# High halves of the weight tiles: a rounding DMA from GpSimd in place of a GpSimd instruction

## The chip, the cores and the metric

One core of one Trainium2 chip runs the whole program. The metric is the device time of one execution in microseconds; the median of several runs is compared. A profile is one more execution, recorded instruction by instruction.

## What is computed

One layer of a streaming encoder, for 512 prompt tokens and 32 sample tokens together (544 columns, model width 1024):

```python
z = rmsnorm(x, n1) @ w_in              # 52 tiles of 128 features: q, k, v of mixers A and B, gates
mixed = sigmoid(ga) * attend_A(...) + sigmoid(gb) * attend_B(...)   # 16 heads each
x = x + mixed @ w_out
u = rmsnorm(x, n2) @ w_up              # 2 x 2816 features
a, g = split(causal_conv3(u))
x = x + (gelu(a) * g) @ w_down
```

All of it is float32, and the products have to keep most of float32's precision.

## The kernel before

Each weight matrix is cut into tiles of 128 rows by 1024 columns (eight blocks of 128 by 128): 52 tiles of `w_in`, 8 of `w_out`, 44 of `w_up` and 22 of `w_down`, 126 in all, used one after the other in a fixed order. TensorE takes operands of a rounded type (float32r). To keep precision each operand is split into a high half (the value rounded) and a low half (the rest), and one block of weights costs three products: high weights with high activations, high weights with low activations, low weights with high activations (`triple`). With two column halves of 272 and eight blocks, one weight tile is 48 products.

`prep(n)` makes the two halves of tile n. SyncE (its queue is SP) loads the tile into `w_raw`; GpSimd (POOL in the profile) multiplies it by one into `w_hi`, whose type rounds (L193); VectorE (DVE) subtracts to get `w_lo` (L194). There are two buffers each of `w_raw`, `w_hi` and `w_lo`. So `w_hi` of tile n can be written only when TensorE has read the high half of tile n-2 for the last time, and TensorE can start tile n only when the new half is there:

```python
raw = wp.tile([128, 1024], F32, name="w_raw", bufs=2)
hi = wp.tile([128, 1024], F32R, name="w_hi")
lo = wp.tile([128, 1024], F32R, name="w_lo")
```

`weights()` takes the next tile and has up to two further ones prepared ahead of it in program order. The first two tiles come in two pieces each.

The program has four stages. In the first, tiles of `w_in` are projected while heads of both mixers, in steps, are woven between the products by the class `Stream`; every step of a head has work on ScalarE (ACT), VectorE and GpSimd, GpSimd doing the normalization of the softmax (L483) and the squares of the head norms (L403, L404, L411). Then come `w_out`, `w_up` (with a convolution per tile: L925, L932, L937 on VectorE, and four instructions of one or two columns on GpSimd, L928 to L935) and `w_down`. Within each engine the instructions stand in the order that a list scheduler gave them when the program was built; at run time each engine takes them strictly in that order, and an instruction that waits holds up everything behind it on its engine.

Of the kernel before, what the change touches and what calls it, by code (L numbers as in the profile page):

```python
# [11 lines left out]
ALU = mybir.AluOpType  # L12
# [3 lines left out]
NP = 512                 # prompt tokens  # L16
NS = 32                  # sample tokens
T = NP + NS              # columns of the activations
# [4 lines left out]
CA = 128                 # cached keys of mixer A  # L23
CB = 256                 # cached keys of mixer B
FF = 2816
UT = 2 * FF // 128       # tiles of the up projection
# [3 lines left out]
A_BLK = 80               # sample keys of mixer A: 2 blocks of 80 (32 new, 128 cached)  # L30
B_BLK = 96               # sample keys of mixer B: 3 blocks of 96 (32 new, 256 cached)
LN_EXP = "natural_log_exp_and_others"

# tiles of w_in, 128 output features each
QA, KA, VA, QB, KB, VB, GA, GB = 0, 8, 10, 12, 20, 28, 36, 44

# columns of the packed per-feature vectors
# [11 lines left out]
# how long the operands of a task's next step take, in the units of Stream.clock  # L49
LAT_FIRST, LAT_ROW = 9.15, 0.35          # the norm of the columns, before w_in and before w_up  # L50
LAT_SQ, LAT_NORM, LAT_DMA = 2.9, 6.89, 3.63
LAT_Z, LAT_SOFT, LAT_PT = 6.55, 9.34, 4.75
LAT_SOFT_S, LAT_PTS = 8.46, 1.1          # the sample's
PACE_A, PACE_B, PACE_S = 7.09, 5.87, 1.44

WARM = 7                 # products that bring the tensor engine's clock up
START = "x0a w0 x0b x1 w1 x2 w0 x3 w1 x4 x5 x6 x7"   # first loads: rows of x (or halves), parts of w
FIRST = 3                # tiles of w_in whose products go ahead of the norm
RESCALE = 8              # tiles of w_in whose moving operand is without the norm
GATES_B = (1, 2, 12, 12)  # before which group of A (0-3) or pair of B (4-11) the gates of B come  # L60
LATER = -300             # the priority of work that others can go ahead of


class Stream:
    """The order of the tensor engine's work: products are queued as they are emitted, and tasks
    (generators that yield how long their next step's operands take) resume between them.  Heads
    wait in a queue until their projections are there, one of them starting every PACE."""
# [24 lines left out]
    def queue(self, fetch, start, needs, pace, ahead=0):  # L92
        """a head: what to load ahead, the task, and when its operands are there; it goes
        before the last `ahead` ones"""
        self.heads.insert(len(self.heads) - ahead, [fetch, start, needs, None, pace])
        self.prefetch()

    def reserve(self, name, n, limit):
        """let tasks go on until n more of a group of buffers can be had"""
        while self.live.get(name, 0) + n > limit:  # L100
            self.idle()
        self.live[name] = self.live.get(name, 0) + n
# [15 lines left out]
    def step(self):  # L118
        """resume one task whose operands are there, or start a head"""
# [19 lines left out]
def body(ctx, tc, a, o):  # L139
# [21 lines left out]
    def load(out, src, kind="x"):  # L161
        """loads of a kind are issued in the order in which they are asked for"""
        with tc.issue_after(loads[kind].ins) if kind in loads else nullcontext():
            loads[kind] = nc.sync.dma_start(out=out, in_=src)

    # ---------------------------------------------------------------- weights
# [18 lines left out]
    def prep(n):  # L185
# [5 lines left out]
        for c in map(slice, cuts, cuts[1:]):  # L191
            load(raw[:, c], sources[n][:, c])
            G.tensor_scalar(hi[:, c], raw[:, c], 1.0, 1.0, ALU.mult, ALU.mult)  # L193
# [16 lines left out]
    def triple(ps, w, k, c0, cn, first, last):  # L210
        """the products of one block of weights: high x high, high x low, low x high"""
# [27 lines left out]
    def rescale(n, s, k):  # L239
        """the columns' norm goes into the moving operand: the tiles after RESCALE have it"""  # L240
# [13 lines left out]
    def interleaved(halves, ks):  # L254
        """row by row"""
# [5 lines left out]
    def dense_first(evac):  # L261
        """the first tiles of a stage: their products start as the rows come in, and they
        leave their banks when the norm of the columns is there"""
# [13 lines left out]
    def leave(z, ps, c0, cn):  # L277
        """from a bank, with the norm if the moving operand was without it"""
# [5 lines left out]
    # -------------------------------------------------------------- constants  # L284
# [16 lines left out]
    # ------------------------------------------------------------------ norms  # L301
    def newton(st, cn, pool):
        """(b - 3) y = -2 / sqrt(st + eps)"""
# [16 lines left out]
    class RowNorm:  # L320
        """the reciprocal root mean square of every column, of rows that come one by one"""
# [38 lines left out]
    # products without a use, until the first rows are there: they bring the clock up  # L360
# [29 lines left out]
    # -------------------------------------------------------- projected tiles  # L390
# [38 lines left out]
    def load_q(stacks, sample, ready):  # L429
        """stacks: per head of the pair a [128, 512] tile of high and low halves"""  # L430
# [11 lines left out]
    def load_v(vt, vs, cached, vt_out, c_out, ready):  # L442
        """vt[token, tile, head, (high, low), feature]; vs[key, block, head, feature] for the sample"""
# [23 lines left out]
    # -------------------------------------------------------------- attention  # L467
    def softmax(p, tiles, mx, sinkcol):
        """tiles: slices of p holding scores whose row maxima are the columns of mx"""
# [24 lines left out]
    def transposed(p, blocks, n):  # L494
        """blocks: (column in p, column in the result); returns high and low parts of p^T"""
# [609 lines left out]
```

## Time and profile before

| | us |
|---|---|
| median of 3 runs | 934.55 (932.86 to 937.06) |
| span of the profiled execution, first to last instruction | 931.9 |
| TensorE products busy | 905.8 (97%) |
| TensorE weight loads busy | 891.7 (96%) |
| VectorE busy | 656.7 (70%) |
| GpSimd busy | 467.0 (50%) |
| ScalarE busy | 445.1 (48%) |

The profiled execution's own time is its span, 931.9 us; what a run has around the span is not recorded for it, and the median of the runs is 2.65 us above it. Busy time of TensorE is the time in which at least one product is under way; products overlap one another, so a busy TensorE need not be one at its full rate. Only idle time of the engine that sets the end counts; the other engines' idle time costs nothing by itself.

### The profile page before, as it was taken

How to read it: one execution, taken by the hardware profiler on the slowest of the kernel's cores; microseconds unless marked ns; L12 is line 12 of the kernel's file. 1: busy time of each engine (PE TensorE's matmuls, PEld its weight loads, DVE VectorE, ACT ScalarE, POOL GpSimd, SP SyncE). 2: the span in 40 equal slices, each digit the busy share in tenths (PEclk: the TensorE clock that was granted, in tenths of full speed). 3: DMA queues.
4: the chain of work that ended last, by engine and by line, in shares of the span. 5: the costliest groups of instructions: out<-in, count | busy, mean ns of one | idle time of the engine just before them, and what ended most of it. 6: DMA issues, size and time to landing. Idle time of an engine off the chain costs nothing.

```text
span 931.9 us, 18669 instructions
## 1 busy us (share of the span) xinstructions
PE 905.8 (97%) x7181; PEld 891.7 (96%) x7181; DVE 656.7 (70%) x1243; ACT 445.1 (48%) x1103; POOL 467.0 (50%) x636
## 2 busy tenths in 40 slices
PE   7979999999999999999999999999999999999998
PEld 6878999989989999999999999999999999999998
DVE  7798867777988988989766568777777777422221
ACT  5667887778878687777672232222222222000000
POOL 5625548366777677766451146544555554311110
PEclk9999999999999999999999999999999999999999
DMA  6222123312344344334324222222222222333321
GB/s 220 89 91 83 52 95 99 103 59 83 109 145 128 98 138 128 127 110 125 107 86 169 89 70 91 91 91 91 91 84 80 87 92 91 107 103 103 113 90 40
DMA packets 39000, 94.35 MB, mean 101 GB/s; under 512 B 4832, under 2 KB 14336, under 8 KB 38912
## 3 DMA queue, kind: packets, MB, share of 16 engines
q1 hardware_dynamic: 38912, 93.17, 31.1%
q8 instruction: 56, 0.92, 0.4%
q14 instruction: 32, 0.26, 0.1%
HBM read 80.48 MB, written 7.10 MB: 94 GB/s over the span
## 4 chain that ended last, share of the span: by engine, by line
PE 78%; DVE 8%; ACT 3%; POOL 3%; issue 2%; DMA 0%; DVEq 0%; POOLq 0%; ACTq 0%
PE ps L80 75%; PE ps L84 3%; DVE q L436 1%; ACT p L475 1%; DVE w_lo L194 1%; DVE p L491 1%; POOL p L483 1%; DVE zn L412 1%; DVE s L244 1%; DVE t_b L309 1%; POOL t_sql L404 1%; DVE k L421 0%; POOL z L411 0%; DVE xl L317 0%; DMA k<-k 0%
## 5 line engine op out<-in xcount | busy, mean ns | idle before, releaser
L80 PE MATMUL ps<-xh,w_lo 128*128 128x272 f32 x1536 | 444.4, 290 | 5.9 <-DVE w_lo L194 5.8
L80 PE MATMUL ps<-xh,w_hi 128*128 128x272 f32 x1536 | 444.1, 291 | 3.4 <-ACT z L402 1.6
L80 PE MATMUL ps<-xl,w_hi 128*128 128x272 f32 x1536 | 444.2, 290 | 1.3 <-DVE xl L317 1.2
L80 PEld LDWEIGHTS ps<-xh,w_lo 128*128 128x128 f32 x1536 | 289.4, 189 | 7.6 <-DVE w_lo L194 7.0
L80 PEld LDWEIGHTS ps<-xh,w_hi 128*128 128x128 f32 x1536 | 289.7, 189 | 4.9 <-ACT z L402 1.9
L80 PEld LDWEIGHTS ps<-xl,w_hi 128*128 128x128 f32 x1536 | 289.8, 189 | 2.6 <-DVE xl L317 2.1
L193 POOL TENSOR_SCALAR w_hi<-w_raw 128x1024 fp32r<-128x1024 f32 (+2 forms) x128 | 137.5, 1074 | 288.8 <-PE ps L80 178.2
L194 DVE TENSOR_TENSOR w_lo<-w_raw,w_hi 128x1024 fp32r<-128x1024 f32 (+2 forms) x128 | 162.4, 1270 | 105.6 <-POOL w_hi L193 105.2
L80 PE MATMUL ps<-s,w_hi 128*128 128x272 f32 x960 | 180.6, 288 | 0.0
L80 PEld LDWEIGHTS ps<-s,w_hi 128*128 128x128 f32 x960 | 150.4, 188 | 0.0
L80 PE MATMUL ps<-s,w_lo 128*128 128x272 f32 x480 | 137.8, 288 | 0.0
L483 POOL TENSOR_SCALAR p<-p,rc 128x256 f32<-128x256 f32 (+3 forms) x128 | 74.5, 598 | 43.3 <-DVE rc L481 39.9
L80 PEld LDWEIGHTS ps<-s,w_lo 128*128 128x128 f32 x480 | 90.2, 188 | 0.0
L475 ACT ACTIVATE p<-p,nm 128x256 f32<-128x256 f32 (+3 forms) x128 | 65.4, 513 | 27.8 <-DVE nm L472 27.7
L925 DVE TENSOR_TENSOR u<-ps,rstd 128x272 f32<-128x272 f32 x88 | 38.2, 438 | 38.8 <-PE ps L80 38.2
L420 ACT CAST s<-s 128x544 fp32r<-128x544 f32 x30 | 19.4, 647 | 84.9 <-DVE s L950 81.5
L80 PE MATMUL ps<-k,q 128*128 128x256 f32 (+2 forms) x256 | 52.1, 308 | 3.3 <-DMA k<-k 1.6
L404 POOL TENSOR_TENSOR t_sql<-t_sq,t_sqh 128x272 fp32r<-128x272 f32 x52 | 52.6, 1011 | 3.7
L411 POOL TENSOR_TENSOR z<-z,t_y 128x272 f32<-128x272 f32 x52 | 42.6, 821 | 21.9 <-ACT t_y L306 19.9
L931 ACT ACTIVATE s<-u,cols 128x544 f32<-128x544 f32 x44 | 36.9, 842 | 34.0 <-DVE u L925 34.0
L945 ACT ACTIVATE s<-s 128x544 f32<-128x544 f32 x22 | 14.5, 658 | 75.5 <-DVE s L937 75.5
L403 POOL TENSOR_SCALAR t_sqh<-t_sq 128x272 fp32r<-128x272 f32 x52 | 29.9, 575 | 39.4 <-ACT t_sq L401 34.7
(129 smaller groups left out, 1340.9 us busy)
## 6 DMA issues: line engine op xcount, KB each, us to landing
w_raw<-in_w_in SPq DMA_DIRECT2D x50, 512.0 KB, 3.3
w_raw<-in_w_up SPq DMA_DIRECT2D x44, 512.0 KB, 3.2
w_raw<-in_w_down SPq DMA_DIRECT2D x22, 512.0 KB, 3.2
k<-k SPq DMA_DIRECT2D x40, 128.0 KB, 2.3
bias<-in_rel SPq DMA_DIRECT2D x16, 256.0 KB, 2.7
w_raw<-in_w_out SPq DMA_DIRECT2D x8, 512.0 KB, 3.3
s<-in_x SPq DMA_DIRECT2D x15, 272.0 KB, 5.6
out_vb<-s SPq DMA_DIRECT2D x8, 272.0 KB, 2.3
```

Of the source, the lines that this page charges most:

```text
L80: return self.nc.tensor.matmul(out, lhsT=lhsT, rhs=rhs, **kw)
L84: return self.nc.tensor.transpose(out, src, ident)
L193: G.tensor_scalar(hi[:, c], raw[:, c], 1.0, 1.0, ALU.mult, ALU.mult)
L194: V.tensor_tensor(lo[:, c], raw[:, c], rr(hi)[:, c], ALU.subtract)
L403: G.tensor_scalar(sqh, sq, 1.0, 1.0, ALU.mult, ALU.mult)
L404: G.tensor_tensor(sql, sq, rr(sqh), ALU.subtract)
L411: G.tensor_tensor(z, z, y, ALU.mult)
L420: nc.scalar.copy(dst_hi, src)
L475: act(p[:, sl], p[:, sl], AF.Exp, bias=nm[:, t:t + 1], accum_out=sm[:, t:t + 1])
L483: G.tensor_scalar(p[:, sl], p[:, sl], rc[:, t:t + 1], 1.0, ALU.mult, ALU.mult)
L925: V.tensor_tensor(u[:, 2 + c0:2 + c0 + cn], ps, rstd2[:, c0:c0 + cn], ALU.mult)
L931: act(c, u[:, 0:T], AF.Identity, scale=col("cw0", m), bias=col("cb", m))
```

## The change

`load` gets an argument for the issuing engine. For every tile from the fifth on (`CAST = 4`), `w_hi` is no longer computed by GpSimd from `w_raw`: a second DMA, issued from GpSimd, reads the same tile from memory again and writes it into `w_hi`, rounding to float32r on the way. The DMAs of this kind keep their order among themselves. VectorE's subtraction is as before and now waits for the second DMA in place of the GpSimd instruction. The first four tiles are untouched (six GpSimd instructions, two whole and four in pieces). The diff's other lines only take out comments, so from line 200 on the changed kernel's line numbers are 4 higher, and TensorE's products (L80) stand one line lower.

```diff
+CAST = 4
...
-    def load(out, src, kind="x"):
+    def load(out, src, kind="x", e=nc.sync):
         with tc.issue_after(loads[kind].ins) if kind in loads else nullcontext():
-            loads[kind] = nc.sync.dma_start(out=out, in_=src)
+            loads[kind] = e.dma_start(out=out, in_=src)
...
             load(raw[:, c], sources[n][:, c])
-            G.tensor_scalar(hi[:, c], raw[:, c], 1.0, 1.0, ALU.mult, ALU.mult)
+            if n < CAST:
+                G.tensor_scalar(hi[:, c], raw[:, c], 1.0, 1.0, ALU.mult, ALU.mult)
+            else:
+                load(hi[:, c], sources[n][:, c], "cast", G)
             V.tensor_tensor(lo[:, c], raw[:, c], rr(hi)[:, c], ALU.subtract)
```

The scheduler places instructions anew. In the stage of `w_up`, on VectorE, the order before is this (`u` is the evacuated product of one tile, in two halves; two `u` buffers take turns; L932 and L937 are the convolution):

```order
1087 L925 TENSOR_TENSOR u_8049<-ps,rstd 128x272
1088 L194 TENSOR_TENSOR w_lo<-w_raw,w_hi 128x1024
1089 L932 SCALAR_TENSOR_TENSOR s<-u_8049,cols,s 128x544
1090 L925 TENSOR_TENSOR u_8048<-ps,rstd 128x272
1091 L937 SCALAR_TENSOR_TENSOR s<-u_8049,cols,s 128x544
1092 L950 TENSOR_TENSOR s<-s 128x544
1093 L925 TENSOR_TENSOR u_8048<-ps,rstd 128x272
```

The same place with the change:

```order
1087 L929 TENSOR_TENSOR u_8048<-ps,rstd 128x272
1088 L936 SCALAR_TENSOR_TENSOR s<-u_8048,cols,s 128x544
1089 L929 TENSOR_TENSOR u_8049<-ps,rstd 128x272
1090 L941 SCALAR_TENSOR_TENSOR s<-u_8048,cols,s 128x544
1091 L198 TENSOR_TENSOR w_lo<-w_raw,w_hi 128x1024
1092 L929 TENSOR_TENSOR u_8049<-ps,rstd 128x272
```

Before, `w_lo` stood right behind the second half of a tile's `u`; with the change it stands behind the first half of the next tile's `u` and just ahead of that tile's second half.

On GpSimd, in the first stage, the order before is this (L483 is the softmax's normalization, four instructions a head):

```order
60 L193 TENSOR_SCALAR w_hi<-w_raw 128x1024
61 L411 TENSOR_TENSOR z<-z,t_y 128x272
62 L483 TENSOR_SCALAR p<-p,rc 128x128
63 L483 TENSOR_SCALAR p<-p,rc 128x256 x3
64 L193 TENSOR_SCALAR w_hi<-w_raw 128x1024
65 L483 TENSOR_SCALAR p<-p,rc 128x128
66 L483 TENSOR_SCALAR p<-p,rc 128x256 x3
67 L193 TENSOR_SCALAR w_hi<-w_raw 128x1024
```

And with the change:

```order
62 L165 DMA w_hi<-in_w_in 128x1024
63 L487 TENSOR_SCALAR p<-p,rc 128x128
64 L487 TENSOR_SCALAR p<-p,rc 128x256 x3
65 L487 TENSOR_SCALAR p<-p,rc 128x128
66 L487 TENSOR_SCALAR p<-p,rc 128x256 x3
67 L165 DMA w_hi<-in_w_in 128x1024
```

The DMA takes the place of the instruction in GpSimd's order, with other work behind it as before. In all 122 instructions of 128x1024 become 122 DMAs; the number of instructions on the other engines is the same.

## Rows read from the trace of the kernel before

**Rows 1.** The page: busy tenths and granted clock, in 40 slices of the span.
```profile
PE   7979999999999999999999999999999999999998
...
PEclk9999999999999999999999999999999999999999
```

**Rows 2.** Stages (first, w_out, w_up, w_down): stretch, length, each engine's busy us (instructions), clock, DMA.
```profile
0.00:100.00 100.00, 85.81 (x621) 80.99 (x622) 83.94 (x176) 65.74 (x159) 49.38 (x64) 0.98 0.38 119
100.00:476.00 376.00, 367.30 (x2957) 358.38 (x2957) 308.36 (x709) 290.49 (x820) 246.68 (x318) 1.00 0.34 105
476.00:531.00 55.00, 55.00 (x437) 54.82 (x436) 33.45 (x50) 17.65 (x27) 12.39 (x14) 1.00 0.37 128
531.00:803.00 272.00, 272.00 (x2173) 272.00 (x2172) 200.09 (x275) 71.25 (x98) 137.88 (x222) 1.00 0.26 88
803.00:931.90 128.90, 125.72 (x1002) 125.50 (x1000) 30.90 (x36) 0.00 (x0) 20.66 (x20) 1.00 0.27 91
```

**Rows 3.** Waits of TensorE, whole span: us in total, times, longest.
```profile
PE ps L80 <- DVE w_lo L194: 5.8, 3, 3.0
PE ps L80 <- POOL w_hi L193: 2.7, 2, 1.4
```

**Rows 4.** Timeline of GpSimd in w_down: start, us, instruction, idle before and releaser.
```profile
814.23 1.05 POOL L193 TENSOR_SCALAR w_hi<-w_raw 128x1024 fp32r<-128x1024 f32 x1 [4.92 <-PE ps L80]
820.23 1.05 POOL L193 TENSOR_SCALAR w_hi<-w_raw 128x1024 fp32r<-128x1024 f32 x1 [4.95 <-PE ps L80]
```

**Rows 5.** Timeline of VectorE in w_down, the first two and the last of 19 subtractions.
```profile
809.35 1.23 DVE L194 TENSOR_TENSOR w_lo<-w_raw,w_hi 128x1024 fp32r<-128x1024 f32 x1 [4.33 <-POOL w_hi L193]
...
815.32 1.23 DVE L194 TENSOR_TENSOR w_lo<-w_raw,w_hi 128x1024 fp32r<-128x1024 f32 x1 [2.08 <-POOL w_hi L193]
...
917.71 1.23 DVE L194 TENSOR_TENSOR w_lo<-w_raw,w_hi 128x1024 fp32r<-128x1024 f32 x1 [4.09 <-POOL w_hi L193]
```

**Rows 6.** DMA issues: KB each, median us from issue to landing.
```profile
w_raw<-in_w_down SPq DMA_DIRECT2D x22, 512.0 KB, 3.2
k<-k SPq DMA_DIRECT2D x40, 128.0 KB, 2.3
s<-in_x SPq DMA_DIRECT2D x15, 272.0 KB, 5.6
```

**Rows 7.** DMA queue of SyncE: packets, MB, share of 16 engines over the span.
```profile
q1 hardware_dynamic: 38912, 93.17, 31.1%
```

**Rows 8.** Timeline of GpSimd in w_up, about one tile, and the next rounding.
```profile
603.79 1.05 POOL L193 TENSOR_SCALAR w_hi<-w_raw 128x1024 fp32r<-128x1024 f32 x1 [1.97 <-issue]
604.81 0.19 POOL L928 TENSOR_SCALAR state_u<-u 128x2 f32<-128x2 f32 x1
604.96 1.19 POOL L929 TENSOR_SCALAR state_u<-u 128x2 f32<-128x2 f32 x1
...
609.81 1.05 POOL L193 TENSOR_SCALAR w_hi<-w_raw 128x1024 fp32r<-128x1024 f32 x1 [2.41 <-issue]
```

**Rows 9.** Timeline of VectorE in w_up, the same tile and the next, and one L421 of w_down's start.
```profile
604.88 1.23 DVE L194 TENSOR_TENSOR w_lo<-w_raw,w_hi 128x1024 fp32r<-128x1024 f32 x1 [0.63 <-POOL w_hi L193]
606.83 0.44 DVE L925 TENSOR_TENSOR u<-ps,rstd 128x272 f32<-128x272 f32 x1
607.43 0.79 DVE L937 SCALAR_TENSOR_TENSOR s<-u,cols,s 128x544 f32<-128x544 f32 x1 [0.16 <-POOL s L935]
610.18 1.24 DVE L421 TENSOR_TENSOR s<-s 128x544 fp32r<-128x544 f32 x1
...
802.12 0.73 DVE L421 TENSOR_TENSOR s<-s 128x544 fp32r<-128x544 f32 x1 [0.71 <-ACT s L420]
```

**Rows 10.** The GpSimd instructions that go, by stretch (0 to 100, 100 to 476): busy us (count).
```profile
0.00:100.00 100.00, 14.70 (x14) 0.98 0.38 119
100.00:476.00 376.00, 44.83 (x41) 1.00 0.34 105
```

**Rows 11.** Waits of VectorE in the first stage: us in total, times, longest.
```profile
DVE w_lo L194 <- POOL w_hi L193: 9.4, 10, 1.5
```

## The prediction

> **What bounds the kernel now.** I read the page's slices first, then the stages, then who waits for whom, and last the timeline of single weight tiles, because the change acts once per tile. The slices show TensorE at 9 tenths nearly everywhere, with dips only in the first tenth of the span, at a granted clock of full speed (2.4 GHz of the two levels) [rows 1]. The table by stage says where anything can still be won: from 476 to 803 us TensorE is busy for the whole of its stretch (55.00 of 55.00, 272.00 of 272.00), and w_down's 3.2 us of idleness are the output behind the last product; before 476 us it stands idle for 14.2 us in the first 100 and for 8.7 us in the next 376, some 23 in all, while VectorE is busy for 84% and 82% of the same stretches [rows 2]. Of these waits only 8.5 us name a half of the weights [rows 3], so at most a percent hangs on the preparation of weights as it is.
>
> **The beat of a tile.** In w_down nothing but weights moves, so the beat is clean there. GpSimd's rounding starts at 814.23 and 820.23, each time released by TensorE, which has just read the high half of the tile two back [rows 4]. VectorE's subtractions run from 809.35 to 917.71, 18 periods on: 108.36 / 18 = 6.02 us a tile [rows 5]. That is 48 products of 0.125 us, so TensorE sets the beat. Within it the preparation takes 1.05 us (rounding from 814.23), 0.04 us, and 1.23 us (subtraction from 815.32): it is done at 816.55, and TensorE needs it only when it gets to that tile, at about 820.2, for the low half two products of 0.125 us later, 820.45. **The slack is 3.9 us per tile.**
>
> **What is removed.** 122 GpSimd instructions of 128x1024 go. In the last three stages they are worth nothing: their cover is the tile TensorE is working on, with the 3.9 us just found. In the first stage 55 of them stand, 59.5 us; six small and whole ones of the first four tiles stay, about 6 us, so GpSimd loses some 53 us of work there [rows 10]. What that can give back is bounded below by nothing (GpSimd is busy for 296 of 476 us, so it is no bound) and above by the 8.7 us that TensorE idles after 100 us, plus little of the 14.2 before, which are mostly the first loads and the first four tiles, unchanged [rows 2]. A second gain is VectorE's: a subtraction of 128x544 took 1.24 us beside GpSimd's rounding (610.18; the rounding had begun at 609.81) and 0.73 us alone (802.12) [rows 8, 9]. Without rounding beside it VectorE runs such instructions faster.
>
> **What is added.** In its place comes a chain per tile: TensorE releases the buffer, GpSimd issues, the DMA lands, VectorE subtracts. Call X the time from release to landing; before, 1.05 us stood there. No row shows a DMA issued from GpSimd or one that rounds, so X is bounded from neighbours. From below: the same 512 KB from SyncE's queue take 3.2 us from issue to landing [rows 6], so X is 3.2. From above: GpSimd's own part could be as long as the longest small instruction there, 1.19 us, and the transfer can share the engines with the `w_raw` load of a later tile, which now starts when VectorE has subtracted, late in the period. A transfer's size costs (3.2 - 2.3) us for 384 KB [rows 6], so 512 KB move in about 1.2 us, and two that meet fully stretch each other by that: X = 3.2 + 1.2 + 1.2 = 5.6. Deep crowding is dearer: 5.6 us for only 272 KB when the rows of x and the first tiles come in together [rows 6]; but the queue moved data for 31.1% of the span [rows 7], the change adds 64 MB to its 93.17 and brings that to about 52%, so such crowding should stay at the start. I take X = 3.2 + 1.05, the issue priced as the instruction whose place it takes, which is the nearest row: **X = 4.25 us.**
>
> Only a page prices the issue: the Trainium skill, "DMA: Bandwidth & Descriptors", section Specifications, puts the first byte at about 1 us from GpSimd against about 0.6 us from SyncE. By that X would be 3.2 + 0.4 = 3.6, and the sum would be the same; no row here shows it.
>
> **Where X starts to cost.** In w_down the high half's buffer is free at about 814.15, and the low half is needed at 820.45; with 1.23 for the subtraction and 0.07 for the hand-overs, X may be 820.45 - 814.15 - 1.30 = 5.0 us. Beyond it, since a tile's buffer is that of two tiles back, a cycle of two tiles lengthens by the excess: **(X - 5.0) / 2 per tile**. At 4.25 the low half is ready 0.75 us early: nothing for the 8 + 44 + 22 = 74 tiles of the last three stages.
>
> In w_up VectorE is also the queue that the wait moves through. Before, the subtraction stood right behind a tile's second half of `u`; the new order puts it behind the next tile's first half, three microseconds on, and ahead of that tile's second half. With the release at T it reaches the head at about T + 4.2 (the half at T + 3.0, 0.44 for it, 0.79 for L937 [rows 9]), ends at T + 5.5, and `u` is due at T + 6.0: it waits for nobody and nobody waits for it. GpSimd's issue stands where the instruction stood, and behind it the same four small instructions, due later.
>
> In the first stage the 48 later tiles of w_in come every 476 / 52 = 9.2 us on average, so the new 3.2 us (4.25 - 1.05) fit on average, but VectorE takes its instructions in order: it stood for `w_hi` 10 times, 9.4 us in all [rows 11], and where the scheduler has not moved the subtraction far enough these waits grow. Against it stands the relief of GpSimd and VectorE. I set the two against each other: nothing. The SyncE queue is untouched but for the order of a few issues; the second read competes with the key copies (2.3 us each [rows 6]), a few tenths at most on the path.
>
> **Sum.** Span 931.9 + 0 (first stage, gain against wait) + 0 (w_out) + 0 (w_up) + 0 (w_down) = 931.9; with the 2.65 us by which the median of the runs stands above this span, 934.5. I say 935.
>
> **The rivals.** *The chain becomes the beat* (slower). If issue and landing take more than 5.0 us, the dense stages run at (X + 7.0) / 2 instead of 6.02. At the upper bound of 5.6 that is 0.3 us a tile, 74 tiles, 22 us, and a few of w_in's dense runs with it, say 28: 963. For it: two 512 KB transfers now move in every 6.02 us, and rounding on the way may slow one. A row shows that GpSimd can also be held up: L929, two columns, took 1.19 us where L928, just like it, took 0.19; it began at 604.96, while VectorE's subtraction ran from 604.88 to 606.11 [rows 8, 9]. If writing a DMA's descriptors were held up like that, 1.2 us would come on top in w_up, X = 5.45, and 44 tiles by 0.22 would give 10 us, 945. The Trainium skill says so in "DMA: Bandwidth & Descriptors", section SWDGE vs HWDGE vs iDMA: GpSimd writes its descriptors into SBUF, and VectorE's two-port mode locks it out there, which DMAs from SyncE do not feel. By that rule the issue would be hit; the trace agrees that small GpSimd instructions are, and no row shows it for a DMA. Against it: in w_down VectorE does nothing between the tiles.
>
> *The first stage gains* (faster). 53 us of GpSimd work and the slowed VectorE instructions beside it go, and heads get through sooner. It can give at most the 8.7 us of idleness after 100 us, with a little of the first 100: 8 us, 926.5. For it: VectorE is over 80% busy there, so faster instructions help. Against: the products woven between hide most of it already.
>
> *VectorE stands for the landing in the first stage* (slower). Ten waits, each longer by 3.2 us, are 32 us of standing on an engine with 476 - 392 = 84 us to spare; if a third of it reaches TensorE, 11 us, 945. It decides as soon as the real landing is later than the scheduler took it for.
>
> That the change does not do what it says is small: the new order has 122 DMAs on GpSimd, and the rounding instruction left only for the first four tiles.
>
> **How the numbers follow.** No change, 930 to 939.5: 0.35, the likeliest single case. The chain as the beat: 0.28. The first stage gains: 0.22. VectorE stands: 0.15. About 0.5%, 4.7 us, is what a measurement of this kernel can tell from no change. So faster 0.22, same 0.35, slower 0.43. The range takes in most of the gain, 925, and goes up to the priced bound of the chain, 963; the likeliest case's own range is 930 to 939.5. Left out are deeper crowding (X of 6.5 would give 56 us) and a gain of more than 1%.
>
> **What would show it.** The landing of the new DMA, issue to landing, of 3 to 4 us with a beat of 6.02 us between w_down's subtractions proves X harmless; TensorE waits on `w_hi` or `w_lo` in w_up and w_down, and a beat above 6.02, prove the first rival. Idle time of TensorE before 476 us tells the other two: under 18 us the gain, above 28 us with VectorE waiting for the DMA the loss. L421 at 0.73 us and L929 at 0.19 would show who disturbed whom. The forecast is wrong if the end of the first stage moves by more than 5 us, or if w_up and w_down together last longer than 403 us.

## The result and the profile after

The changed kernel takes **966.56 us** (median of 4 runs, 964.60 to 969.22) against 934.97 us (4 runs, 932.86 to 937.06) of the kernel before on the same chip: ratio 1.0344, 95% interval 1.0313 to 1.0376. It is slower by 3.4%. The prediction was 935 us, and its range, up to 963, ends 3.6 us short of the time. The profiled execution has a span of 966.6 us, 34.7 more than before.

The page's slices hardly show it: TensorE is still at 9 tenths, with a few eights [rows 1].

```profile
PE   8989999999999999999989999999999998999998
```

The table by stages, at the edges of [rows 2] (columns: stretch, length, busy us and instructions of TensorE, its weight loads, VectorE, ScalarE, GpSimd; clock, DMA share, GB/s), shows more: TensorE was busy for all of the 55.00 and 272.00 us; now 4.6 and 9.4 us are idle there. GpSimd's load falls (137.88 to 60.30 in the fourth row), as forecast, and the DMA share goes from 0.26 to 0.50.

```profile
0.00:100.00 100.00, 89.34 (x656) 85.15 (x657) 81.13 (x180) 67.72 (x163) 47.22 (x68) 0.98 0.51 161
100.00:476.00 376.00, 363.73 (x2870) 352.64 (x2869) 291.36 (x697) 284.23 (x804) 209.57 (x305) 1.00 0.54 160
476.00:531.00 55.00, 50.39 (x395) 48.66 (x394) 29.97 (x47) 19.24 (x37) 11.66 (x22) 0.97 0.54 175
531.00:803.00 272.00, 262.59 (x2049) 257.64 (x2049) 175.82 (x260) 67.22 (x93) 60.30 (x203) 1.00 0.50 167
803.00:966.60 163.60, 156.00 (x1218) 153.19 (x1217) 49.67 (x63) 6.63 (x9) 16.32 (x40) 1.00 0.51 166
```

These edges no longer fall on the stages, so I measure the stages by VectorE's evacuations: the first one of w_out ends the first stage, and first to last is the length of each later stage.

| kernel | first stage ends | w_out | w_up | w_down |
|---|---|---|---|---|
| before | 492.6 | 38.5 | 252.9 | 116.4 |
| after | 499.1 | 45.0 | 269.2 | 119.7 |
| difference | +6.5 | +6.5 | +16.3 | +3.3 |

That is 32.6 of the 34.7 us; the passage from w_up to w_down takes 1.9 more, the output behind the last evacuation the rest. Half of the loss is w_up's, **0.37 us for each of 44 tiles**. The rows of the evacuations after, w_out, w_up and w_down (line, engine, operation, count, min/median/max ns, first to last start):

```profile
L892 DVE TENSOR_TENSOR s<-ps,s x16: 430/442/443, 499.1 to 544.1; 128x272 f32<-128x272 f32 x16
L929 DVE TENSOR_TENSOR u<-ps,rstd x88: 426/436/443, 556.3 to 825.5; 128x272 f32<-128x272 f32 x88
L988 DVE TENSOR_TENSOR s<-ps,s x16: 432/441/444, 843.6 to 963.3; 128x272 f32<-128x272 f32 x16
```

The mark between the first two columns is uneven. The first four evacuations of w_out start at 492.6, 493.0, 493.5 and 496.5 us before, and at 499.1, 499.5, 499.8 and 500.1 after: the new order finishes the first two tiles of w_out together. TensorE's first product that reads w_out starts at 482.8 before and 486.3 after. By that mark the first stage loses about 3.5 us, and some 3 of its 6.5 belong to the passage into w_out.

TensorE's waits over the whole span (us, times, longest) answer [rows 3]: 8.5 us for a half of the weights have become over 25.

```profile
PE ps L81 <- DVE w_lo L198: 16.4, 27, 3.2
PE ps L81 <- DMA w_hi<-in_w_up: 4.7, 6, 1.3
PE ps L81 <- DMA w_hi<-in_w_out: 4.3, 1, 4.3
```

TensorE's idle time grows from 26.1 to 44.5 us, which is 18.4 of the 34.7. The rest hides in its busy time: in w_up a product starts every 0.125 us and counts as busy for 0.29, so a short pause shows as no idleness. From the first to the last evacuation of w_up 54 products start more than 0.14 us after the one before them, where the kernel before has none, and these pauses add 16.7 us, which is the whole loss of w_up.

What the subtractions wait for on VectorE answers [rows 11]:

```profile
DVE w_lo L198 <- DMA w_hi<-in_w_down: 59.9, 16, 6.5
DVE w_lo L198 <- DMA w_hi<-in_w_up: 36.2, 29, 5.2
DVE w_lo L198 <- DMA w_hi<-in_w_in: 33.4, 24, 3.4
```

The DMA issues (queue, count, KB, median us from issue to landing) answer [rows 6]. The medians of the new DMA are 4.2 to 4.8 us, and the old ones have grown too: the raw loads of w_down from 3.2 to 3.9, the key copies from 2.3 to 4.8. The queues answer [rows 7]: GpSimd's adds 63.97 MB.

```profile
q1 hardware_dynamic: 38912, 93.17, 29.7%
q0 software_dynamic: 17568, 63.97, 21.7%
...
w_hi<-in_w_in POOLq DMA_DIRECT2D x48, 512.0 KB, 4.2
...
w_hi<-in_w_up POOLq DMA_DIRECT2D x44, 512.0 KB, 4.8
w_raw<-in_w_down SPq DMA_DIRECT2D x22, 512.0 KB, 3.9
w_hi<-in_w_down POOLq DMA_DIRECT2D x22, 512.0 KB, 4.4
k<-k SPq DMA_DIRECT2D x40, 128.0 KB, 4.8
```

The timeline of w_down shows the chain tile by tile. GpSimd, to be held against [rows 4]:

```profile
862.95 0.53 POOL L165 DMA_DIRECT2D w_hi<-in_w_down  x1 [5.48 <-PE ps L81]
868.96 0.53 POOL L165 DMA_DIRECT2D w_hi<-in_w_down  x1 [5.48 <-PE ps L81]
```

and VectorE, against [rows 5] (the first, two in the middle, the last of 19):

```profile
842.49 1.23 DVE L198 TENSOR_TENSOR w_lo<-w_raw,w_hi 128x1024 fp32r<-128x1024 f32 x1 [4.82 <-DMA w_hi<-in_w_down]
...
868.44 1.22 DVE L198 TENSOR_TENSOR w_lo<-w_raw,w_hi 128x1024 fp32r<-128x1024 f32 x1 [6.54 <-DMA w_hi<-in_w_down]
872.82 1.23 DVE L198 TENSOR_TENSOR w_lo<-w_raw,w_hi 128x1024 fp32r<-128x1024 f32 x1 [3.16 <-DMA w_hi<-in_w_down]
...
955.41 1.23 DVE L198 TENSOR_TENSOR w_lo<-w_raw,w_hi 128x1024 fp32r<-128x1024 f32 x1 [5.66 <-DMA w_hi<-in_w_down]
```

Issuing costs GpSimd 0.53 us here. From issue to subtraction it is 5.49 us for the first tile (862.95 to 868.44) and 3.86 for the second (868.96 to 872.82). The time is not constant, and it goes with where the raw load of another tile starts. These are SyncE's raw loads beside the two issues:

```profile
861.92 1.37 SPq L165 DMA_DIRECT2D w_raw<-in_w_down  x1
...
869.69 0.33 SPq L165 DMA_DIRECT2D w_raw<-in_w_down  x1
```

The first was issued 1.03 us ahead of the high half's DMA, the second 0.73 us behind it. No DMA of w_up and w_down travels alone: a raw load is under way during each of the 66. In nine of them no raw load starts between 2.0 us before and 1.2 us after the issue, and these land in 3.46 to 3.78 us; the other 57 take 3.45 to 7.11, with a median of 4.8. The beat of the 19 subtractions is (955.41 - 842.49) / 18 = 6.27 us where it was 6.02.

Why the two meet: SyncE's raw load waits for the subtraction that empties its buffer, as its row of waits says. A late subtraction starts the raw load late, close to the next high-half DMA. In the 5.6 us after the first of the two issues both queues moved their 512 KB (0.54 and 0.52 MB, share of the 16 engines), and each landing took over 5 us:

```profile
SPq L165 <- DVE w_lo L198: 460.3, 93, 11.0
```

```profile
q1 hardware_dynamic: 153, 0.54, 36.0%
q0 software_dynamic: 144, 0.52, 25.3%
...
w_raw<-in_w_down SPq DMA_DIRECT2D x1, 512.0 KB, 5.1
w_hi<-in_w_down POOLq DMA_DIRECT2D x1, 512.0 KB, 5.3
```

### The profile page after: what moved, and what is told of

It reads as the page before. It is cut to its first block, busy times and chain, and to the rows that moved or that the text cites. A ratio compares the mean times of both kernels' runs of the same rounds, so it can differ in the third digit from the quotient of the medians.

```text
span 966.6 us, 18776 instructions
## 1 busy us (share of the span) xinstructions
PE 922.1 (95%) x7181; PEld 897.3 (93%) x7181; DVE 628.0 (65%) x1243; ACT 445.0 (46%) x1103; POOL 345.1 (36%) x636
## 3 DMA queue, kind: packets, MB, share of 16 engines
q0 software_dynamic: 17568, 63.97, 21.7%
## 4 chain that ended last, share of the span: by engine, by line
PE 39%; DMA 20%; DVE 14%; issue 13%; ACT 8%; POOL 6%; SPq 0%; DVEq 0%; POOLq 0%; ACTq 0%
PE ps L81 37%; DMA w_hi<-in_w_up 8%; DVE w_lo L198 5%; DMA w_hi<-in_w_in 5%; DMA w_hi<-in_w_down 4%; ACT p L479 2%; POOL p L487 2%; DVE p L495 2%; DMA w_hi<-in_w_out 2%; PE ps L85 1%; POOL z L415 1%; DVE q L440 1%; DVE zn L416 1%; POOL t_sql L408 1%; DVE xl L321 1%
## 5 line engine op out<-in xcount | busy, mean ns | idle before, releaser
L81 PE MATMUL ps<-s,w_lo 128*128 128x272 f32 x480 | 133.6, 292 | 2.9 <-DVE w_lo L198 2.6
L487 POOL TENSOR_SCALAR p<-p,rc 128x256 f32<-128x256 f32 (+3 forms) x128 | 72.0, 576 | 53.0 <-DVE rc L485 40.8
L165 POOL DMA_DIRECT2D w_hi<-in_w_up x44 | 25.2, 572 | 138.9 <-PE ps L81 138.9
L81 PE MATMUL ps<-k,q 128*128 128x256 f32 (+2 forms) x256 | 54.4, 311 | 3.7 <-DVE v L459 1.7
L936 DVE SCALAR_TENSOR_TENSOR s<-u,cols,s 128x544 f32<-128x544 f32 x44 | 34.4, 784 | 35.7 <-ACT s L935 35.7
L165 POOL DMA_DIRECT2D w_hi<-in_w_down x22 | 11.8, 535 | 118.9 <-PE ps L81 99.7
L506 DVE TENSOR_TENSOR pt_l<-ps,pt_h 128x512 fp32r<-128x512 f32 (+1 forms) x80 | 45.9, 603 | 8.1 <-ACT pt_h L505 6.9
L85 PE MATMUL ps<-ident,p 128*128 128x128 f32 x272 | 46.9, 277 | 4.1 <-POOL p L487 3.9
```

The lines of the kernel that those rows point to most:

```text
L81: return self.nc.tensor.matmul(out, lhsT=lhsT, rhs=rhs, **kw)
L85: return self.nc.tensor.transpose(out, src, ident)
L165: loads[kind] = e.dma_start(out=out, in_=src)
L487: G.tensor_scalar(p[:, sl], p[:, sl], rc[:, t:t + 1], 1.0, ALU.mult, ALU.mult)
L506: V.tensor_tensor(l[:, :n], ps[:, :n], rr(h)[:, :n], ALU.subtract)
L936: V.scalar_tensor_tensor(c, u[:, 1:T + 1], col("cw1", m), c, ALU.mult, ALU.add)
```

## The experiments

The theory after the result: in the dense stages the chain of a two-buffer tile (release, issue, landing, subtraction) is longer than TensorE's work, because the landing is stretched by the raw load. The rivals: the bytes themselves, the rounding on the way, GpSimd's issue, the new order of the instructions. All stage times in one table, columns as above; the ratio is to the kernel before, with its 95% interval (a single run has none). The stage times are read from one profiled execution of each kernel, and runs of one kernel differ by up to 5 us (e11: 939.72 to 944.71).

| kernel | us | ratio | first stage ends | w_out | w_up | w_down |
|---|---|---|---|---|---|---|
| e1_first | 942.40 | 1.0077 [1.0054, 1.0100] | 501.1 | 39.0 | 253.0 | 116.3 |
| e2_last | 961.87 | 1.0291 [1.0266, 1.0315] | 494.2 | 47.5 | 262.8 | 119.1 |
| e3_hi3 | 944.52 | 1.0106 [1.0085, 1.0128] | 499.8 | 43.5 | 254.2 | 116.5 |
| e4_traffic | 955.01 | single run | 491.8 | 42.4 | 268.8 | 116.3 |
| e5_noraw | 943.16 | single run | 494.8 | 44.2 | 253.3 | 116.8 |
| e6_traffic2 | 934.76 | 1.0002 [0.9985, 1.0019] | 492.4 | 38.5 | 253.0 | 116.3 |
| e7_hi3all | 942.72 | 1.0087 [1.0072, 1.0102] | 501.6 | 38.1 | 253.9 | 116.6 |
| e8_cut | 938.26 | 1.0040 [1.0028, 1.0052] | 497.1 | 38.5 | 252.9 | 116.4 |
| e9_early13 | 936.19 | 1.0023 [1.0010, 1.0036] | 495.6 | 38.5 | 253.0 | 116.3 |
| e10_early9 | 934.78 | 1.0008 [0.9997, 1.0020] | 494.0 | 38.5 | 253.0 | 116.3 |
| e11_mid | 944.04 | 1.0093 [1.0066, 1.0119] | 502.3 | 39.1 | 253.0 | 116.3 |
| e12_traf1 | 961.76 | 1.0287 [1.0266, 1.0308] | 520.6 | 38.5 | 252.9 | 116.4 |
| e13_traf_sp | 945.12 | 1.0111 [1.0091, 1.0131] | 505.5 | 38.5 | 252.9 | 116.4 |
| e14_cut_after | 970.32 | 1.0387 [1.0363, 1.0411] | 502.3 | 44.7 | 265.6 | 121.7 |

### The two halves of the program apart

e1_first has the DMA for the tiles of the first stage alone:

```diff
-            if n < CAST:
+            if n < CAST or n >= 52:
```

> The DMA only for the later 48 tiles of w_in; w_out, w_up and w_down round on GpSimd as before. Theory A (the chain from buffer release over landing to subtraction has become the beat of the dense stages): those stages return to 6.02 us a tile, and what is left is the first stage's 3 to 7 us: 938 to 942 us. Theory B (the second read of every tile slows everything in proportion to its bytes): 48 of 122 DMAs, so 48/122 of 32 us, 947 us. Theory C (the loss is made in the first stage by VectorE standing for landings): nearly all of it stays, 960 us or more.

e2_last has it for the tiles from w_out on:

```diff
-CAST = 4
+CAST = 52
```

> The complement: GpSimd rounds all tiles of w_in, the DMA brings w_out, w_up and w_down. Theory A: 934.5 plus 26 to 30 us, 960 to 965. Theory B: 74/122 of 32 us, 954. Theory C: under 940.

Each half keeps its own loss: e1 is 0.8% slower, e2 2.9%. In e1, w_up and w_down without the DMA are back within 0.1 us (w_out within 0.5); in e2 the first stage ends at 494.2, 1.6 after before. Four fifths of the loss belongs to the dense stages.

### A third buffer

e3_hi3 gives the high halves from tile 56 on a third buffer, so that a DMA may start a tile earlier:

```diff
...
-        hi = wp.tile([128, 1024], F32R, name="w_hi")
+        third = n >= 56 and n % 3 == 2
+        hi = (more[0] if third else wp).tile([128, 1024], F32R, name="w_hi3" if third else "w_hi")
...
+    more.append(att.enter_context(tc.tile_pool(name="wx", bufs=1)))
```

> The changed kernel with a third buffer for the high half from tile 56 on (the fifth of w_out), where the memory has room; the DMA of a tile is then released one tile earlier, at the same traffic and with the same waits on VectorE. Theory A: w_up and w_down return to 6.02 us a tile, their loss of 21 us goes, and 942 to 948 us are left. Theory B and theory C: nothing changes, 963 to 968.

w_up and w_down return to 254.2 and 116.5 us. VectorE now waits for TensorE's release of the low half and not for a landing, at a beat of 6.0 us:

```profile
832.84 1.23 DVE L199 TENSOR_TENSOR w_lo<-w_raw,w_hi 128x1024 fp32r<-128x1024 f32 x1 [4.79 <-PE ps L81]
838.88 1.23 DVE L199 TENSOR_TENSOR w_lo<-w_raw,w_hi 128x1024 fp32r<-128x1024 f32 x1 [4.82 <-PE ps L81]
```

So the chain was the beat in both stages: with the same DMAs and the same bytes, one more buffer takes 18 of the 19.6 us back. In w_up e3 changes a second thing: the scheduler puts nearly every subtraction (41 of 43) right behind a half of `u`, so that there the new order is not ruled out by this run alone. In w_down VectorE has nothing but subtractions and evacuations in all of these kernels, in nearly the same order, and there the third buffer's effect stands alone.

### The bytes, the rounding and the meeting

e4_traffic is the kernel before, with DMAs of the same bytes from GpSimd into tiles that nobody reads, from tile 56 on; even ones round to float32r, odd ones copy:

```diff
...
             G.tensor_scalar(hi[:, c], raw[:, c], 1.0, 1.0, ALU.mult, ALU.mult)
+            if n >= 56:
+                kind = "plain" if n % 2 else "round"
+                load(more[0].tile([128, 1024], F32 if n % 2 else F32R, name=kind), sources[n], "cast", G)
```

> The kernel before with the DMA added from tile 56 on into a tile that nobody reads, rounding for even tiles and plain for odd ones; GpSimd still rounds. It has all the traffic and GpSimd's issue in w_up and w_down, but no chain. Theory A: 934 to 938 us. Theory B: 70/122 of 32 us, 952. If rounding on the way costs time, the landing of the even ones is longer than that of the odd ones by over 0.3 us; theory A does not need it.

955.0 us, and w_up at 268.8: by the number alone the bytes would carry the loss. The waits of GpSimd (us, times, longest) say that the experiment made a wait of its own: the scheduler put the DMAs far ahead, and GpSimd stood for the landing of the one two back, with its rounding behind it.

```profile
POOL round L165 <- DMA round<-in_w_up: 25.5, 13, 3.8
```

That was not the question, so e6 below puts it anew. e5_noraw is the changed kernel without the raw loads from tile 56 on; the subtraction reads an old raw tile there, so the true low halves of the last four tiles of w_out and of all of w_up and w_down are left out:

```diff
...
-            load(raw[:, c], sources[n][:, c])
+            if n < 56:
+                load(raw[:, c], sources[n][:, c])
```

> The changed kernel without the w_raw load from tile 56 on: the subtraction there reads an old tile, so the low halves of the later tiles are left out of the computation, and the DMA that rounds has the engines to itself. Theory A1 (only the meeting of the two loads makes the chain too long): its landing falls below 4.0 us, w_up and w_down return to 6.02 us a tile, 943 to 948 us in all. Theory A2 (issue and landing are too long even alone): the landing stays over 4.4 us and the time at 960 us or more.

The beat is back with two buffers (253.3 and 116.8), and the DMA lands in 3.5 to 3.6 us:

```profile
w_hi<-in_w_up POOLq DMA_DIRECT2D x44, 512.0 KB, 3.6
w_hi<-in_w_down POOLq DMA_DIRECT2D x22, 512.0 KB, 3.5
```

e6_traffic2 is e4 with each DMA kept behind the rounding of its tile:

```diff
...
+                spare = more[0].tile([128, 1024], F32 if n % 2 else F32R, name=kind)
+                with tc.issue_after(rounded.ins):
+                    G.dma_start(out=spare, in_=sources[n])
```

> e4 mended: each added DMA is issued right behind the rounding instruction of its tile, so they go one per tile and GpSimd does not stand for a landing two tiles back. Theory A: the bytes alone cost nothing, 934 to 938 us. Theory B: 70/122 of 32 us, 952. Rounding DMAs land within 0.3 us of plain ones.

934.76 us, ratio 1.0002 [0.9985, 1.0019]: no cost that can be told, with the bytes of the changed kernel from tile 56 on.

```profile
w_raw<-in_w_up SPq DMA_DIRECT2D x44, 512.0 KB, 4.4
round<-in_w_up POOLq DMA_DIRECT2D x22, 512.0 KB, 3.6
plain<-in_w_up POOLq DMA_DIRECT2D x22, 512.0 KB, 3.6
```

Three things follow. The bytes cost nothing, even with the raw load at 4.4 us in place of 3.2, so the raw load has slack. The rounding costs nothing: 3.6 us with it, 3.6 without. And what does cost is a DMA **in the chain** that meets another one closely: take away the other load (e5) or the chain (e6), and the loss is gone. e6 also moves the meeting: none of its 66 DMAs of w_up and w_down has a raw load starting between 2.0 us before and 1.2 us after its issue, so it does not show what a close meeting without a chain would do.

### The first stage

e7_hi3all has three buffers of high halves for all tiles; to make room, `t_o` has one buffer and `z` three. e8_cut is the kernel before with the same cuts, e14_cut_after the changed kernel with them.

```diff
-        hi = wp.tile([128, 1024], F32R, name="w_hi")
+        hi = wp.tile([128, 1024], F32R, name="w_hi", bufs=3)
...
-            z = ap.tile([128, 272], F32, name="z", bufs=4)[:, :cn]
+            z = ap.tile([128, 272], F32, name="z", bufs=3)[:, :cn]
...
-        t = ap.tile([128, 512], F32, name="t_o", bufs=2)
+        t = ap.tile([128, 512], F32, name="t_o", bufs=1)
```

> A third high-half buffer for all tiles; room from one buffer less of t_o and of z. Theory A: w_out, w_up and w_down at 6.02 us a tile, and in the first stage VectorE's 33 us of standing for landings shrink below 12 us, so the first stage is within 2 us of the control's: 930 to 938 us beside the control. Theory D (the first stage loses to later key copies, which land after 4.8 us instead of 2.3, or to the new order): the first stage still loses 5 to 8 us, 940 to 943 us.

> The control of e7: the kernel before with the same two buffers less. Both theories: 934 to 938 us; if it is above, e7 is read against it.

> The changed kernel with the same two cuts (one t_o buffer and one z buffer fewer), two w_hi buffers as in the change. Against e7, which has the third buffer, it shows what the standing of VectorE for landings is worth in the first stage. Theory (standing costs, the rest is order): first evacuation of w_out at 503 to 507 us against e7's 501.6, and 968 to 974 us in all. Rival (standing costs nothing, the whole loss of the first stage is the order): first evacuation of w_out at 500.5 to 502.5 us, 966 to 969 us in all.

The cuts alone cost 4.5 us of the first stage (492.6 to 497.1). With the DMA it ends 5.2 us after the control's (502.3), and a third buffer takes 0.7 of that back (501.6). So small a difference lies within what one execution can tell. Yet the third buffer does away with the standing: in e14 the subtractions of the first stage wait for a landing, in e7 there is no such row there, only a short wait for TensorE. First stage of e14, then of e7:

```profile
DVE w_lo L198 <- DMA w_hi<-in_w_in: 20.5, 16, 3.5
```

```profile
DVE w_lo L198 <- PE ps L81: 7.0, 9, 2.0
```

So for the first stage the rival of e14's text fits better (its 502.3 is in that range, while the 970.3 in all falls to the theory's): no gain from ending 20 us of standing on VectorE can be told. By TensorE's first product of w_out the three stand at 487.3 (e8), 488.0 (e14) and 490.0 us (e7): there e14 is only 0.7 us behind its control, and most of its 5.2 us are lost in the passage into w_out. The schedules differ between these three, so none of this is a price of the wait alone. w_out is another matter: 44.7 us in e14, 38.1 in e7. That loss is the missing buffer's.

Where in the first stage the time goes shows in its two parts, before (first fence) and after (second), columns as in [rows 2]:

```profile
0.00:250.00 250.00, 231.63 (x1807) 224.38 (x1808) 201.18 (x459) 184.37 (x492) 141.81 (x190) 0.99 0.32 99
250.00:490.00 240.00, 235.48 (x1879) 228.81 (x1878) 200.77 (x439) 180.42 (x500) 159.23 (x198) 1.00 0.39 118
```

```profile
0.00:250.00 250.00, 236.93 (x1849) 229.29 (x1849) 193.70 (x465) 187.46 (x500) 128.99 (x196) 0.99 0.50 153
250.00:490.00 240.00, 230.03 (x1796) 221.57 (x1797) 186.03 (x424) 173.74 (x487) 133.47 (x187) 0.99 0.56 167
```

For 250 us the changed kernel is ahead, by 42 products (42 x 0.125 = 5 us): the stage does run faster there. In the next 240 us it gets through 83 fewer. Three runs asked whether a part of the first stage could keep the gain: the DMA only for tiles 4 to 12 (e9), 4 to 8 (e10), 13 to 51 (e11).

```diff
-            if n < CAST:
+            if n < CAST or n >= 13:
```

> The DMA for tiles 4 to 12 alone, about the first 100 us, where e1 and the changed kernel had 31 to 34 products more done than the kernel before (655 and 658 against 624 at 100 us). If that head start is kept to the end: 930 to 932 us, faster than both. If what follows is a queue of its own that takes it back: 934 to 936. Theory D for the rest of w_in predicts the former.

> The DMA for tiles 4 to 8 alone: half the head start if it is earned tile by tile, 932 to 934 us; the same as e9 if it is earned in the first tiles.

> The DMA for tiles 13 to 51 alone: the part of the first stage after 100 us. If VectorE standing for landings there costs the first stage its time, the whole loss of e1 and the lost head start: 942 to 946 us. If the first stage loses by something at its start or end, 935 to 938.

None does. e9 and e10 are 0.2% and 0.1% above before (e10's interval takes in 1), e11 loses 0.9% like e1. A head start does not last; no row shows what it is given back to.

Two runs put the doubled reads alone into the first stage. e12_traf1 adds to e8 a rounding DMA per tile from GpSimd into one spare buffer; e13_traf_sp a plain one from SyncE:

```diff
+            if 4 <= n < 52:
+                spare = wp.tile([128, 1024], F32, name="spare", bufs=1)
+                load(spare, sources[n], "spare")
```

> The control e8 (1.0040 of the kernel before) with a rounding DMA per tile added for tiles 4 to 51, issued behind the GpSimd rounding of its tile into one spare buffer that nobody reads: the first stage's bytes, GpSimd issues and later key copies, without a chain and with VectorE's order of before. If the key copies and the bytes are what the first stage loses by: 1.009 or more of the kernel before, with key copies landing after 4 us. If it is what VectorE waits for and the order that comes with it: 1.003 to 1.005, whatever the key copies' landing.

> The kernel before with the two cuts of the control (938.3 us, first evacuation of w_out at 497.1 us), and beside each of the tiles 4 to 51 a second, plain read of the same 512 KB into a spare buffer that nobody reads, issued from SyncE. The order of instructions on TensorE, VectorE, ScalarE and GpSimd is the control's, row for row; only SyncE's queue has 48 more rows. Theory (the first stage is lost to VectorE standing for landings and to the new order, the bytes are harmless): 937 to 940 us, first evacuation of w_out at 496 to 498.5 us, though the key copies go up from 2.3 towards 4.8 us. Rival (the doubled reads hold up key copies and raw loads, and that is what the first stage pays): 941 to 945 us, first evacuation of w_out at 500 to 504 us, with TensorE or VectorE waiting more for k<-k or w_raw. SyncE may itself stand for the spare buffer; if its own waits exceed 30 us the run says less.

e12 fits neither expectation: the scheduler made another order with it, and what TensorE waits for most has nothing to do with weights (8.3 us for VectorE's `pt_l`), at a mean granted clock of 0.984. It says little of the reads.

e13 has the control's order, row for row on every engine but SyncE, and by its end (505.5) it would speak for the rival. But SyncE stood 119.2 us for the spare buffer, far over the 30 named in its text, and a key copy was queued behind: one wait of TensorE of 4.5 us between 170 and 180 us, where the mean granted clock is 0.81. SyncE's and TensorE's waits of e13:

```profile
SPq L164 <- DMA spare<-in_w_in: 119.2, 43, 5.4
```

```profile
PE ps L80 <- DMA k<-k: 6.0, 2, 4.5
```

The stretch ahead of that stall can be read. For 170 us e13 moves 217 GB/s and its control 103, and TensorE gets through the same work; e13, then e8:

```profile
0.00:170.00 170.00, 153.64 (x1148) 146.98 (x1149) 131.31 (x284) 117.15 (x296) 87.78 (x115) 0.97 0.64 217
170.00:180.00 10.00, 4.68 (x24) 4.10 (x23) 3.55 (x6) 2.35 (x7) 3.12 (x4) 0.81 0.57 164
```

```profile
0.00:170.00 170.00, 154.18 (x1151) 147.49 (x1152) 132.68 (x287) 118.74 (x301) 90.12 (x118) 0.97 0.33 103
```

1148 products against 1151: twice the reads cost TensorE nothing there. Since the orders are the same, the two can be held against each other product by product: e13 is 0.3 us behind its control at 164 us, 7.6 behind from 203 to 400 us, and 8.4 at the end of the stage. The one stall makes up most of its loss. But SyncE ran ahead with the added reads: the last of the 48 was issued at 202.9 us, and from 200 to 400 us e13 moves 116 GB/s where its control moves 110. So the run says nothing of doubled reads after 250 us, where the changed kernel loses.

What is left for that part is the reads there, the new order of the instructions, and when the landings come in. The order and the reads do not set the loss by themselves: the changed kernel, e3 and e5 have the same order on all engines and the same transfers up to there, and in the one execution that is profiled of each the first product of w_out starts at 486.3, 487.1 and 482.0 us, the last of these 0.8 us ahead of the kernel before. **This part stays open.**

No version beat the kernel before; e6 and e10 equal it.

## Why the prediction was wrong

**The step that failed is X.** The prediction took 4.25 us from release to landing, put the meeting with the raw load into the upper bound only, and so found X harmless with 0.75 us to spare below 5.0. Measured from release to landing, X has a median of 4.97 us in w_up, where 21 of 44 lie above 5.0, and of 4.60 in w_down, where 7 of 22 do. The limit itself fits: with landings of 3.5 to 3.6 (e5) the stages run at their old beat. The formula with a single X does not: by w_down's median it gives no loss, and the beat was 6.27 us. The cycle behind it does, taken tile by tile: if a buffer comes free 6.02 us after the last one or 7.0 us plus X after the last but one, whichever is later, the measured X give 6.32 us a tile in w_up and 6.29 in w_down, and the buffers came free every 6.38 and 6.35 us. What failed is the choice between the two ends:

- *The issue was priced too high.* 1.05 us was taken; GpSimd is busy for 0.53 to 0.60, once for 0.74. Alone, the whole of issue and landing is 3.5 to 3.6, so X was 0.7 too high for a DMA that travels alone. The estimate from the Trainium skill's figures ("DMA: Bandwidth & Descriptors", section Specifications) was 3.6, and the rows of e5 and e6 agree.
- *The meeting is the rule, not the bound.* The prediction had named the raw load "which now starts when VectorE has subtracted, late in the period", and did not follow it round the cycle. By its own X the subtraction ends 4.25 + 1.30 = 5.55 us after the release, and the next high half is released at 6.02: the raw load starts half a microsecond ahead of it. Then a long landing makes the subtraction late, and that the raw load. 57 of 66 met closely. The bound from [rows 6] for it, 5.6 us, was near the 5.1 and 5.3 of the two shown above, but the longest landing took 7.1.
- *A median is not the price.* The landing after has a median of 4.4 us in w_down, under the threshold. Long and short ones take turns in no fixed order (3.5 to 6.4 us there), and TensorE takes the tiles in order, so that a short one does not pay back a long one: this is the "whichever is later" in the reckoning above.

**The rival that came true** is the chain as the beat, given 0.28 and priced at 28 us, 963. Its mechanism is shown by e3, e5 and e6 together with the reckoning tile by tile. Its size, 0.3 us a tile, was 0.37 in w_up and less in w_down (3.3 us for 22 tiles); that the whole came so near 963 is partly luck, since w_out lost far more than its eight tiles' share and the first stage for a reason that is not known.

**w_up: the queue on VectorE.** The prediction let the subtraction wait for nobody. In the trace the two places take turns: one subtraction stands idle for its DMA (694.70), the next ran straight behind L954 (700.64), 6.13 us after its DMA was issued at 694.51.

```profile
694.70 1.23 DVE L198 TENSOR_TENSOR w_lo<-w_raw,w_hi 128x1024 fp32r<-128x1024 f32 x1 [1.93 <-DMA w_hi<-in_w_up]
...
700.01 0.72 DVE L954 TENSOR_TENSOR s<-s 128x544 f32<-128x544 f32 x1
700.64 1.22 DVE L198 TENSOR_TENSOR w_lo<-w_raw,w_hi 128x1024 fp32r<-128x1024 f32 x1
```

The order fence ahead of the prediction showed one of the two patterns, and the argument was made for that one alone. It cost little: with the start of each subtraction in place of its landing, the reckoning above gives 6.33 us a tile in w_up against 6.32.

**w_out was set to nothing** with the other dense stages. It lost as much as the first stage. In the new order its first two tiles end together, so nothing covers the chain of the third. The buffer for that tile's high half was released at 499.32, the DMA was issued at 499.49 and landed at 503.94; TensorE's last product before it ended at 499.80, and TensorE idled for 4.3 us. Before, the rounding there ran from 492.81 to 493.86 and TensorE had work until 495.0. The rows of x come in at the same time, with the 16 engines at 0.97, but they can account for no more than the 0.9 us by which this landing (4.46) exceeds 3.6.

```profile
495.00:500.00 5.00, 4.81 (x39) 4.59 (x37) 2.01 (x5) 0.73 (x2) 0.51 (x1) 1.00 0.97 346
500.00:505.00 5.00, 0.92 (x4) 0.73 (x4) 3.18 (x5) 2.40 (x4) 0.61 (x2) 0.93 0.81 276
505.00:510.00 5.00, 4.85 (x30) 4.75 (x30) 2.40 (x4) 0.00 (x0) 0.00 (x0) 0.72 0.63 202
```

The prediction had the row for it, 5.6 us for 272 KB among the rows of x [rows 6], and held that "such crowding should stay at the start". Eight of that row's 15 loads start at 485.8 to 489.5 us, at w_out.

**The first stage.** VectorE stood 33.4 us for landings, 24 times, where 32 were forecast for ten waits. Whether a third of it reaches TensorE, as that rival said, is not shown; the stage lost 6.5 us by the first evacuation, 3.5 by the first product of w_out, against the 11 it gave. The gain was there for 250 us and went again. The sign was that of the rival; its cause is open.

**GpSimd held up by VectorE** (10 us, 945): not seen. In w_down three issues that lie wholly beside a subtraction (849.79, 920.05 and 944.95) took 0.53 us, like those with nothing beside them (862.95); in w_up such issues took 0.58 (568.69, 714.07), again like the rest. The rule that the prediction took from the Trainium skill ("DMA: Bandwidth & Descriptors", section SWDGE vs HWDGE vs iDMA) is about VectorE's two-port mode. The prediction took it that the subtraction runs in that mode; no row shows it, and the issues speak against a hold-up. The small instructions are faster: GpSimd's L929, two columns, median 1.17 us before, takes 0.18 now (L933). Before, 40 of the 44 ran beside a subtraction, now none does, so that is the new order's doing. VectorE's of 128x544 (L421, now L425) takes 0.72 where its median was 1.24. Both lie off the path in w_up and bought nothing.

## What to carry to other kernels

When an instruction inside a cycle of two buffers is replaced by a DMA, price the time from the release of a buffer to the landing, with the other transfers that the same cycle starts beside it, and follow the meeting round the cycle, tile by tile: 57 of 66 met closely here. Give such a DMA a third buffer first, so that its landing is off the cycle; the bytes themselves then cost next to nothing (254.2 and 116.5 us against 252.9 and 116.4). And look at the start of each stage: where both buffers come free together, nothing covers the landing.

## What the hardware showed that was not expected

- A DMA that rounds float32 to float32r on the way lands as fast as a plain one, 3.6 us for 512 KB. From GpSimd it takes 0.3 to 0.4 us more (e5, e6) than from SyncE (3.2, before).
- Two transfers of 512 KB that start close to each other can stretch each other, in the case shown to 5.1 and 5.3 us. Most of it is the start: by the packet records, that high half's first packet came 2.6 us after its issue began, and 1.23 to 1.31 us after it in 64 of the 66 landings of e5, which have no company. In e6, where they start farther apart, GpSimd's DMA keeps its 3.6 us and the raw load takes 4.4.
- A single idle stretch of TensorE of 4.3 us cost more than itself: the mean granted clock was 0.93 and 0.72 in the two stretches of 5 us from its start, as TensorE ran for a while at 1.2 GHz, the lower of its two levels, once it resumed; 30 products ran in the second of them, 39 in the 5 us ahead of the stall. That is 1.8 us on top (an estimate: 5 us by 0.07 and by 0.28). In the 10 us around the 4.5 us wait of e13 the mean was 0.81.
- The key copies, 128 KB from SyncE, went from 2.3 to 4.8 us in the changed kernel, and were at 2.8 in e14, which has the same DMAs, and at 3.6 in e5, which has the changed kernel's order too: neither the bytes nor the order alone sets them.
